# A two-layer diffusion backbone on one core: half vectors of the modulation turned four at a time, and a second top-16 selection over 112 candidates with larger lookups

## The chip, the cores and the metric

One core of a Trainium2 chip runs the whole network as one program. The metric is the device time of one execution in microseconds (us). Three executions of the kernel before took 3133.66, 3143.14 and 3145.10 us; their median is 3143.14 us. One more execution was profiled.

## The reference, cut to what matters

Two layers work on 256 noisy tokens (x) and 256 context tokens, each 1024 wide, in float32. Each layer is a modulated norm, an input projection, three token mixers with gates and an output projection, and then a modulated norm and an expert layer (PEER). Two parts matter here.

The **modulation**: a vector of 6 x 1024 values for each of the two conditioning vectors (x and context).

```python
def _modulation(cvec, w_mod, b_mod):
    m = jax.nn.silu(cvec) @ w_mod + b_mod
    return jnp.split(m[:, None, :], 6, axis=-1)
```

The **routing** of the expert layer: for each token and each of 8 heads two top-16 lists of 128 keys (the first selection), then the top 16 of the 16 x 16 sums of both lists (the second selection), whose places are looked up in the two lists of indices.

```python
    sv, si = lax.top_k(s, PEER_TOPK)
    cand = (sv[..., 0, :, None] + sv[..., 1, None, :]).reshape(B, L, PEER_HEADS, PEER_TOPK * PEER_TOPK)
    cidx = (si[..., 0, :, None] * N_KEYS + si[..., 1, None, :]).reshape(B, L, PEER_HEADS, PEER_TOPK * PEER_TOPK)
    top_s, pos = lax.top_k(cand, PEER_TOPK)
    eidx = jnp.take_along_axis(cidx, pos, axis=-1)
    gate = jax.nn.softmax(top_s, axis=-1)
```

Both lists are sorted from large to small. A pair (a, b) with (a+1)(b+1) > 16 has at least 16 pairs that are no smaller, so the 16 best lie among the pairs with a < 4 (4 x 16 = 64) and those with a >= 4 and b < 4 (12 x 4 = 48).

## The kernel before, in words

The program is a list of Python generators that are stepped against each other; a tile framework then gives every instruction its place on its engine and every tile its buffer, in the order of the program as far as the data are ready. A tile that is asked for while all buffers of its tag are held waits for one to come free. The pool of tag `f2` has 15 buffers of 2 KB per partition (line 66); it holds small weights (`wraw`, line 73: the DFT, pooling, query and key matrices that `front` loads), attention tiles, the one-hot tiles `e` of `gates`, the split activations of the experts and the padded vectors of the modulation. `f1` has 6 buffers of 1 KB.

Every large weight comes by DMA as a 256 KB piece (`raw`), ScalarE (ACT) rounds it to a high half (line 83), and VectorE (DVE) subtracts to get the low half (line 84); TensorE (PE) makes each product as three (lines 93 to 95).

**Modulation** (`mod_steps`, line 169). For each of the 6 parts and each half of 512 columns, 16 products (lines 183, 184) of a padded 128 x 128 tile, of which 4 columns are used (the high and low halves of two conditioning vectors), give 4 rows of 512. ACT copies the 4 rows (line 190). One half later `mod_out` (line 195) turns them into columns: 4 products with a 4 x 2 matrix (line 199, each shown as two records), an add of the bias (line 201), and for two parts one more operation (line 205). There are 24 halves in all: 4 before the first norm, 8 during the first front, 2 before the first expert layer, 4 during it and 6 around the last front.

**Fronts.** `front` (line 359) is a token mixer: a start with products of the loaded small matrices, 8 heads of attention (line 423 on), then two projections. It runs three times: (0,0) for the context, (0,1) for x of layer 0, (1,1) for layer 1. Inside each head it steps a generator `extra` six times. That is the modulation in fronts (0,0) and (1,1), and the routing of the context tokens (`early_routes`, line 930: two second selections) in front (0,1).

**Routing.** `scores` (line 514) makes the key scores and the first selections (`top16` on 128 values). `topk` (line 556) is the second selection for 128 tokens; it runs six times. For each of the 8 heads it makes 256 sums (line 562), and `top16` (lines 549 to 554) does MAX8, FIND_INDEX8 and MATCH_REPLACE8, then MAX8 and FIND_INDEX8 again, over all 256; each index or replace operation is preceded by a small MATCH_VALUE_LOAD. Then, for both lists (w) and four groups of 32 choices, three operations look up the index: compare with 0..15 (line 586), multiply by the list (line 589), sum over the 16 places (line 591). `topk` yields twice for each head and once for each of the 8 lookups, 24 times.

`routes` (line 939), once for each layer, weaves `topk` and `gates` (one-hot products that spread the gates over the experts: lines 628, 632 on DVE, 638 on PE) with `early`, which does a part of the experts' first products ahead of time (`down`, line 701: 24 products, two splits on DVE) at fixed rates per yield (0.36, 0.26, 0.22 and 0.53, 0.40, 0.32 products of 128 experts). The expert layers (`experts_both`, `experts_one`) follow.

Of the kernel before, what the change touches and what calls it, by code (L numbers as in the profile page):

```python
# [22 lines left out]
NH = 8  # L23
# [18 lines left out]
class Net:  # L42
# [22 lines left out]
    def f2(self, shape, dt=F32):  # L65
        return self.f.tile(shape, dt, name="f2", tag="f2", bufs=15)
# [36 lines left out]
    def setup(self):  # L103
        nc, c, h = self.nc, self.c, self.h

        def ld(name, shape):
            t = c.tile(shape, F32, name=name)
            nc.sync.dma_start(t, h[name])
            return t

        self.cv = ld("cv", [128, 8, 2])
        self.bmod = ld("bmod", [128, 2, 6, 8])
        self.hH = c.tile([128, 8, TT], F32R, name="hH")
        self.hL = c.tile([128, 8, TT], F32R, name="hL")
        self.ckvn = c.tile([128, TT], F32, name="ckvn")
        self.kr = c.tile([128, TT], F32, name="kr")

        z = c.tile([128, 8, 4], F32, name="z")
        sg = c.tile([128, 8, 2], F32, name="sg")
        nc.scalar.activation(sg, self.cv, AF.Sigmoid)  # L120
        nc.vector.tensor_mul(z[:, :, 0:2], sg, self.cv)
        sh = c.tile([128, 8, 2], F32R, name="sh")
        nc.vector.tensor_copy(sh, z[:, :, 0:2])
        nc.vector.tensor_sub(z[:, :, 2:4], z[:, :, 0:2], sh.bitcast(F32))
        self.sc4 = c.tile([128, 8, 4], F32, name="sc4")
        nc.vector.tensor_copy(self.sc4, z)
        self.sel = ld("sel", [4, 2])
        for l in range(2):
            self.mods[l] = c.tile([128, 6, 8, 2], F32, name=f"mods{l}")
            for w in (1, 2):  # L130
                self.AB[l, w] = c.tile([128, 8, 2], F32, name=f"ab{l}{w}")
# [12 lines left out]
    def setup2(self):  # L144
# [21 lines left out]
        self.iota16 = c.tile([128, 16], BF, name="iota16b")  # L166
        nc.vector.tensor_copy(self.iota16, it[:, 0:16])

    def mod_steps(self, l, *parts):
        nc, late = self.nc, None  # L170
        for part in parts:
            sc = [self.f2([128, 4, 128], F32R) for _ in range(2)]
            for i in range(2):
                nc.vector.memset(sc[i].bitcast(F32), 0.0)
                nc.vector.tensor_copy(sc[i][:, :, 0:4], self.sc4[:, 4 * i:4 * i + 4, :])
            yield
            for q in range(2):
                p = self.acc([128, 512])
                c0 = part * D + q * 512
                for k in range(8):  # L180
# [4 lines left out]
                    if k == 3 and late:  # L185
                        self.mod_out(l, *late)
                    if k % 2 and k < 7:
                        yield
                m4 = self.f2([4, 512])
                nc.scalar.copy(m4, p[0:4, :])  # L190
                late = part, q, m4
                yield
        self.mod_out(l, *late)

    def mod_out(self, l, part, q, m4):
        nc = self.nc
        mp = self.mm([128, 4, 2])
        for n in range(4):
            nc.tensor.matmul(mp[:, n, :], lhsT=m4[:, n * 128:(n + 1) * 128], rhs=self.sel, start=True, stop=True)
        ns = slice(4 * q, 4 * q + 4)  # L200
        nc.vector.tensor_tensor(self.mods[l][:, part, ns], mp,
                                self.bmod[:, l, part, ns].unsqueeze(2).to_broadcast([128, 4, 2]), op=OP.add)
        if q and part in (1, 4):
            g = self.g1 if part == 1 else self.g2
            nc.vector.scalar_tensor_tensor(self.AB[l, 1 if part == 1 else 2], self.mods[l][:, part], 1.0,
                                           g[:, l, :].unsqueeze(2).to_broadcast([128, 8, 2]),
                                           op0=OP.add, op1=OP.mult)
# [348 lines left out]
    def topk(self, sv, si, out):  # L556
# [3 lines left out]
        for hd in range(NH):  # L560
            cd = self.f1([128, 16, 16])
            nc.vector.tensor_tensor(cd, sv[:, 2 * hd, :].unsqueeze(2).to_broadcast([128, 16, 16]),
                                    sv[:, 2 * hd + 1, :].unsqueeze(1).to_broadcast([128, 16, 16]), op=OP.add)
            scr = self.f1([128, 256])
            yield from self.top16(ts[:, hd, :], pos[:, hd * 16:(hd + 1) * 16], cd.rearrange("p a b -> p (a b)"), scr)
            yield
        sb = kp.tile([128, 16, 16], BF, name="sb", bufs=1)
        nc.vector.tensor_copy(sb, si)
# [7 lines left out]
        pu = kp.tile([128, 2, 128], U32, name="pu", bufs=1)  # L576
        nc.vector.tensor_scalar(pu[:, 0, :], pos, 4, None, op0=OP.logical_shift_right)
        nc.vector.tensor_scalar(pu[:, 1, :], pos, 15, None, op0=OP.bitwise_and)
        pb = kp.tile([128, 2, 128], BF, name="pb", bufs=1)
        nc.vector.tensor_copy(pb, pu)  # L580
        ij = kp.tile([128, 2, 128], F32, name="ij", bufs=1)
        for w in range(2):
            for h2 in range(4):
                ks = slice(32 * h2, 32 * h2 + 32)
                oh = self.f1([128, 32, 16], BF)
                nc.vector.tensor_tensor(oh, self.iota16.unsqueeze(1).to_broadcast([128, 32, 16]),
                                        pb[:, w, ks].unsqueeze(2).to_broadcast([128, 32, 16]), op=OP.is_equal)
                o4 = oh.rearrange("p (h k) a -> p h k a", h=2)
                nc.vector.tensor_tensor(o4, o4, sb[:, 4 * h2 + w:4 * h2 + 4:2, :].unsqueeze(2).to_broadcast(
                    [128, 2, 16, 16]), op=OP.mult)  # L590
                nc.vector.reduce_sum(ij[:, w, ks], oh, axis=AX.X)
# [415 lines left out]
def _constants():  # L1007
# [28 lines left out]
    sel = np.array([[1, 0], [0, 1], [1, 0], [0, 1]])  # L1036
# [66 lines left out]
```

## Time and profile before

| what | value |
|---|---|
| median of three runs | 3143.14 us (3133.66 to 3145.10) |
| the profiled execution's own time | 3146.14 us |
| its span, first to last instruction | 3144.4 us |
| mean granted clock of TensorE | 0.965 |
| busy share of the span: PE, DVE, ACT, POOL | 94%, 81%, 46%, 10% |
| chain that ended last, by engine | PE 65%, DVE 17%, DMA 11%, issue 5%, ACT 2% |

How to read it: a busy share is an average over stages with different limits, so the stages have to be read one by one. The record of a DVE operation overlaps the start of the next one by some 0.08 us (the compare of line 586 has records of 681 ns, and two of them take 1.20 us on the chain); the pieces of the chain of waits show what an operation adds when another one follows it, and those are used for sums. A matmul's record overlaps its neighbours too, so a PE that is shown busy is not PE at its peak.

### The profile page before, as it was taken

To read this page: it belongs to the slowest core of one execution; us is meant where nothing else is said; L and a number is where in the kernel's file an instruction comes from. 1 tells how busy PE (TensorE), PEld (TensorE's weight loads), DVE (VectorE), ACT (ScalarE), POOL (GpSimd) and SP (SyncE) were. 2 spreads that over 40 slices of the span, in tenths; PEclk is the share of its full clock that TensorE was granted. 3 is DMA by queue.
4 is the path that set the end of the run, shared out by engine and by line. 5 is a ranking of instruction groups with operands and counts; after the bars stand their busy time and mean duration, and the time that the engine had idled before them with its cause. 6 is when DMAs were issued, how large, how long until landed. Compare 5 with 4: busy or idle time off the path is not lost.

```text
span 3144.4 us, 55017 instructions
## 1 busy us (share of the span) xinstructions
PE 2945.8 (94%) x19215; PEld 2726.3 (87%) x19215; DVE 2534.3 (81%) x5831; ACT 1460.3 (46%) x2814; POOL 323.9 (10%) x260
## 2 busy tenths in 40 slices
PE   7999899798898999999999999999988889999998
PEld 5799878798888889999999998789877877799997
DVE  6677889798997889899999998566799966666666
ACT  5565444443444443344334434445544544555554
POOL 0000000111000121433333341000000000000000
PEclk8999999899999999999999999999998999999999
DMA  7574443675568878898988986454546788776664
GB/s 233 179 230 142 145 126 111 203 242 194 179 185 251 303 250 273 303 307 305 304 303 304 320 291 214 143 160 142 185 143 186 218 264 278 242 231 205 208 201 141
DMA packets 400719, 695.36 MB, mean 221 GB/s; under 512 B 36793, under 2 KB 148153, under 8 KB 396345
## 3 DMA queue, kind: packets, MB, share of 16 engines
q1 hardware_dynamic: 363576, 557.61, 54.8%
q0 software_dynamic: 36864, 134.23, 12.8%
q8 instruction: 151, 2.47, 0.3%
q14 instruction: 128, 1.04, 0.1%
HBM read 631.94 MB, written 59.77 MB: 220 GB/s over the span
## 4 chain that ended last, share of the span: by engine, by line
PE 65%; DVE 17%; DMA 11%; issue 5%; ACT 2%; SPq 0%; POOL 0%; DVEq 0%; ACTq 0%
PE mm L93 9%; PE mm L94 8%; PE mm L95 8%; PE acc L94 7%; PE acc L95 7%; PE acc L93 7%; DVE wl L84 4%; DMA ge<-E 2%; PE acc L818 2%; PE acc L819 2%; PE acc L817 2%; DVE a L632 2%; DMA raw<-in_up 2%; DMA raw<-in_wmod 1%; DVE f L628 1%
## 5 line engine op out<-in xcount | busy, mean ns | idle before, releaser
L83 ACT CAST wh<-raw 128x512 fp32r<-128x512 f32 x1604 | 981.4, 619 | 1006.4 <-PE acc L95 267.4
L84 DVE TENSOR_TENSOR wl<-raw,wh 128x512 fp32r<-128x512 f32 x1604 | 1075.7, 685 | 276.4 <-ACT wh L83 264.4
L93 PE MATMUL mm<-hH,wh 128*128 128x256 f32 (+1 forms) x2432 | 760.0, 313 | 43.1 <-ACT ge L707 38.9
L94 PE MATMUL mm<-hH,wl 128*128 128x256 f32 (+1 forms) x2432 | 757.1, 311 | 19.8 <-DVE wl L84 18.8
L95 PE MATMUL mm<-hL,wh 128*128 128x256 f32 (+1 forms) x2432 | 751.6, 309 | 0.0
L93 PEld LDWEIGHTS mm<-hH,wh 128*128 128x128 f32 x2432 | 468.3, 193 | 52.2 <-ACT ge L707 44.7
L94 PEld LDWEIGHTS mm<-hH,wl 128*128 128x128 f32 x2432 | 469.3, 193 | 28.6 <-DVE wl L84 25.6
L95 PEld LDWEIGHTS mm<-hL,wh 128*128 128x128 f32 x2432 | 468.7, 193 | 0.0
L94 PE MATMUL acc<-f,wl 128*128 128x384 f32 (+1 forms) x1216 | 402.1, 331 | 7.3 <-DVE wl L84 6.9
L95 PE MATMUL acc<-f,wh 128*128 128x384 f32 (+1 forms) x1216 | 400.4, 330 | 1.9 <-DVE f L731 1.9
L93 PE MATMUL acc<-f,wh 128*128 128x384 f32 (+1 forms) x1216 | 394.1, 330 | 8.0 <-ACT wh L83 2.9
L669 POOL DMA_INDIRECT gx<-in_down,eidx x128 | 184.6, 1442 | 1030.7 <-ACT f L250 573.7
L93 PEld LDWEIGHTS acc<-f,wh 128*128 128x128 f32 x1216 | 230.5, 190 | 14.2 <-issue 6.4
L94 PEld LDWEIGHTS acc<-f,wl 128*128 128x128 f32 x1216 | 232.3, 191 | 11.3 <-DVE wl L84 10.8
L95 PEld LDWEIGHTS acc<-f,wh 128*128 128x128 f32 x1216 | 232.1, 191 | 2.5 <-DVE f L731 2.2
L707 ACT ACTIVATE ge<-mm 128x384 f32<-128x384 f32 (+1 forms) x256 | 111.8, 437 | 241.6 <-PE mm L95 219.6
L728 DVE TENSOR_TENSOR ge<-ge,f 128x256 f32<-128x256 f32 (+1 forms) x384 | 132.6, 375 | 99.5 <-ACT ge L707 50.3
L93 PE MATMUL acc<-hH,wh 128*128 128x256 f32 x688 | 210.4, 306 | 1.3 <-ACT hH L280 1.2
L818 PE MATMUL acc<-wl,f 128*128 128x512 f32 x512 | 202.8, 396 | 7.5 <-DVE wl L84 7.2
L817 PE MATMUL acc<-wh,f 128*128 128x512 f32 x512 | 201.1, 393 | 1.0 <-ACT f L730 1.0
L819 PE MATMUL acc<-wh,f 128*128 128x512 f32 x512 | 200.8, 392 | 0.0
L94 PE MATMUL acc<-hH,wl 128*128 128x256 f32 x688 | 198.6, 289 | 0.1
(207 smaller groups left out, 4496.8 us busy)
## 6 DMA issues: line engine op xcount, KB each, us to landing
raw<-in_downT SPq DMA_DIRECT2D x512, 256.0 KB
raw<-in_up SPq DMA_DIRECT2D x512, 256.0 KB
raw<-in_wmod SPq DMA_DIRECT2D x192, 256.0 KB
raw<-in_winc SPq DMA_DIRECT2D x172, 256.0 KB
G<-f SPq DMA_DIRECT2D x40, 1024.0 KB
f<-G SPq DMA_DIRECT2D x32, 1024.0 KB
raw<-in_wpq SPq DMA_DIRECT2D x96, 256.0 KB
raw<-in_wo SPq DMA_DIRECT2D x48, 256.0 KB
```

Of the source, the lines that this page charges most:

```text
L83: nc.scalar.copy(H, r)
L84: self.last = nc.vector.tensor_sub(L, r, H.bitcast(F32)).ins
L93: t.matmul(out, lhsT=wH, rhs=xH, start=first, stop=False)
L94: t.matmul(out, lhsT=wL, rhs=xH, start=False, stop=False)
L95: t.matmul(out, lhsT=wH, rhs=xL, start=False, stop=last)
L632: nc.vector.tensor_tensor(a, e[:, 0:4].unsqueeze(1).to_broadcast([128, 3, 4, 64, 2]), gT[:, t0 // 4].rearrange("p (x t) d -> p x t d", x=3 ...
L669: nc.gpsimd.indirect_dma_start(out=r, out_offset=None, in_=self.h["up"][0] if up else self.h["down0"], in_offset=bass.IndirectOffsetOnAxis ...
L707: nc.scalar.activation(a, p, AF.Gelu_apprx_tanh)
L728: nc.vector.tensor_mul(y, y, Gg[:, :, c, :])
L817: m(p[t][half], lhsT=aH[:, a], rhs=H[:, 0], start=(i == 0), stop=False)
L818: m(p[t][half], lhsT=aH[:, a], rhs=L[:, 0], start=False, stop=False)
L819: m(p[t][half], lhsT=aL[:, a], rhs=H[:, 0], start=False, stop=(i == 127))
```

## The change

It has two halves.

In the modulation the four used columns are written four times into the padded tile, 32 columns apart, so that the product gives the 4 rows at rows 0, 32, 64 and 96. ACT copies 32 rows of the half's own quarter into one fixed 128 x 512 tile `m4`, and `mod_out` runs once for up to four halves: 4 products with a 128 x 8 selection matrix, then one add for each half. The fixed tile takes the place of one of the 15 `f2` buffers.

In `topk` the 256 sums become 112 (64 + 48) for each head, made for four heads by two operations; `top16` runs over 112. The lookups are made for 64 choices at a time with the 16 places ahead of the choices in memory, so the sum reads with a step of 16 elements. The places come out of the position in 112 by two more shifts and three small operations. The list of indices `sb` is written with every value twice, side by side. The sums, the one-hot tiles and `pu` move from `f1` and the routing pool to `f2`. A yield stands before and after each of the 4 sums, so `topk` still yields 24 times.

```diff
-        return self.f.tile(shape, dt, name="f2", tag="f2", bufs=15)
+        return self.f.tile(shape, dt, name="f2", tag="f2", bufs=14)
...
-        self.sel = ld("sel", [4, 2])
+        self.sel = ld("sel", [128, 8])
+        self.m4 = c.tile([128, 512], F32, name="m4")
+        nc.vector.memset(self.m4, 0.0)
...
-        self.iota16 = c.tile([128, 16], BF, name="iota16b")
-        nc.vector.tensor_copy(self.iota16, it[:, 0:16])
+        self.iota16 = c.tile([128, 16, 16], BF, name="iota16b")
+        nc.vector.tensor_copy(self.iota16, it[:, 0:16].unsqueeze(2).to_broadcast([128, 16, 16]))
...
-                nc.vector.tensor_copy(sc[i][:, :, 0:4], self.sc4[:, 4 * i:4 * i + 4, :])
+                nc.vector.tensor_copy(sc[i].rearrange("p k (r c) -> p k r c", r=4)[:, :, :, 0:4],
+                                      self.sc4[:, 4 * i:4 * i + 4, :].unsqueeze(2).to_broadcast([128, 4, 4, 4]))
...
-                    if k == 3 and late:
-                        self.mod_out(l, *late)
+                    if k == 3 and len(late) == 4:
+                        self.mod_out(l, late)
+                        late = []
...
-                m4 = self.f2([4, 512])
-                nc.scalar.copy(m4, p[0:4, :])
-                late = part, q, m4
+                c = 32 * (len(late) % 4)
+                nc.scalar.copy(self.m4[c:c + 32, :], p[c:c + 32, :])
+                late.append((part, q))
...
-        mp = self.mm([128, 4, 2])
+        mp = self.mm([128, 4, 4, 2])
         for n in range(4):
-            nc.tensor.matmul(mp[:, n, :], lhsT=m4[:, n * 128:(n + 1) * 128], rhs=self.sel, start=True, stop=True)
+            nc.tensor.matmul(mp[:, n].rearrange("p a b -> p (a b)"), lhsT=self.m4[:, n * 128:(n + 1) * 128],
+                             rhs=self.sel, start=True, stop=True)
+        for i, (part, q) in enumerate(halves):
...
-        for hd in range(NH):
-            cd = self.f1([128, 16, 16])
-            nc.vector.tensor_tensor(cd, sv[:, 2 * hd, :].unsqueeze(2).to_broadcast([128, 16, 16]),
-                                    sv[:, 2 * hd + 1, :].unsqueeze(1).to_broadcast([128, 16, 16]), op=OP.add)
-            scr = self.f1([128, 256])
-            yield from self.top16(ts[:, hd, :], pos[:, hd * 16:(hd + 1) * 16], cd.rearrange("p a b -> p (a b)"), scr)
-            yield
-        sb = kp.tile([128, 16, 16], BF, name="sb", bufs=1)
-        nc.vector.tensor_copy(sb, si)
+        for h4 in range(2):
+            cd = self.f2([128, 4, 112])
+            ra, rb = sv[:, 8 * h4:8 * h4 + 8:2, :], sv[:, 8 * h4 + 1:8 * h4 + 8:2, :]
+            nc.vector.tensor_tensor(cd[:, :, 0:64].rearrange("p h (a b) -> p h a b", a=4),
+                                    ra[:, :, 0:4].unsqueeze(3).to_broadcast([128, 4, 4, 16]),
+                                    rb.unsqueeze(2).to_broadcast([128, 4, 4, 16]), op=OP.add)
+            nc.vector.tensor_tensor(cd[:, :, 64:112].rearrange("p h (a b) -> p h a b", a=12),
+                                    ra[:, :, 4:16].unsqueeze(3).to_broadcast([128, 4, 12, 4]),
+                                    rb[:, :, 0:4].unsqueeze(2).to_broadcast([128, 4, 12, 4]), op=OP.add)
+            for i in range(4):
+                hd = 4 * h4 + i
+                scr = self.f1([128, 112])
+                yield from self.top16(ts[:, hd, :], pos[:, hd * 16:(hd + 1) * 16], cd[:, i, :], scr)
+                yield
+        sb = kp.tile([128, 2, 128, 2], BF, name="sb", bufs=1)
+        for d in range(2):
+            nc.vector.tensor_copy(sb.rearrange("p w (h a) d -> p w h a d", h=8)[:, :, :, :, d],
+                                  si.rearrange("p (h w) a -> p w h a", w=2))
...
-        pu = kp.tile([128, 2, 128], U32, name="pu", bufs=1)
+        pu = self.f2([128, 4, 128], U32)
         nc.vector.tensor_scalar(pu[:, 0, :], pos, 4, None, op0=OP.logical_shift_right)
-        nc.vector.tensor_scalar(pu[:, 1, :], pos, 15, None, op0=OP.bitwise_and)
+        nc.vector.tensor_scalar(pu[:, 1, :], pos, 2, None, op0=OP.logical_shift_right)
+        nc.vector.tensor_scalar(pu[:, 2, :], pos, 15, None, op0=OP.bitwise_and)
+        nc.vector.tensor_scalar(pu[:, 3, :], pos, 3, None, op0=OP.bitwise_and)
         pb = kp.tile([128, 2, 128], BF, name="pb", bufs=1)
-        nc.vector.tensor_copy(pb, pu)
+        nc.vector.scalar_tensor_tensor(pb[:, 0, :], pu[:, 1, :], -12.0, pu[:, 0, :], op0=OP.add, op1=OP.max)
+        nc.vector.scalar_tensor_tensor(pb[:, 1, :], pu[:, 0, :], 4.0, pu[:, 2, :], op0=OP.is_lt, op1=OP.mult)
+        nc.vector.tensor_tensor(pb[:, 1, :], pb[:, 1, :], pu[:, 3, :], op=OP.max)
         ij = kp.tile([128, 2, 128], F32, name="ij", bufs=1)
         for w in range(2):
-            for h2 in range(4):
-                ks = slice(32 * h2, 32 * h2 + 32)
-                oh = self.f1([128, 32, 16], BF)
-                nc.vector.tensor_tensor(oh, self.iota16.unsqueeze(1).to_broadcast([128, 32, 16]),
-                                        pb[:, w, ks].unsqueeze(2).to_broadcast([128, 32, 16]), op=OP.is_equal)
-                o4 = oh.rearrange("p (h k) a -> p h k a", h=2)
-                nc.vector.tensor_tensor(o4, o4, sb[:, 4 * h2 + w:4 * h2 + 4:2, :].unsqueeze(2).to_broadcast(
-                    [128, 2, 16, 16]), op=OP.mult)
-                nc.vector.reduce_sum(ij[:, w, ks], oh, axis=AX.X)
+            for h4 in range(2):
+                ks = slice(64 * h4, 64 * h4 + 64)
+                oh = self.f2([128, 4, 16, 16], BF)
+                nc.vector.tensor_tensor(
+                    oh, self.iota16.unsqueeze(1).to_broadcast([128, 4, 16, 16]),
+                    pb[:, w, ks].rearrange("p (h k) -> p h k", h=4).unsqueeze(2).to_broadcast([128, 4, 16, 16]),
+                    op=OP.is_equal)
+                o4 = oh.rearrange("p h a (k d) -> p (h a) k d", d=2)
+                nc.vector.tensor_tensor(o4, o4, sb[:, w, ks, :].unsqueeze(2).to_broadcast([128, 64, 8, 2]), op=OP.mult)
+                yield
+                nc.vector.reduce_sum(ij[:, w, ks].rearrange("p (h k) -> p h k", h=4),
+                                     oh.rearrange("p h a k -> p h k a"), axis=AX.X)
                 yield
```

## Rows read from the trace of the kernel before

**Rows 1.** The page, part 1: busy time and share of each engine.

```profile
PE 2945.8 (94%) x19215; PEld 2726.3 (87%) x19215; DVE 2534.3 (81%) x5831; ACT 1460.3 (46%) x2814; POOL 323.9 (10%) x260
```

**Rows 2.** Busy time by stretch: first front, second front, then four stretches of routing.

```profile
core 0: us, PE busy (x) PEld busy (x) DVE busy (x) ACT busy (x) POOL busy (x), PEclk, DMA share, GB/s
115.00:290.00 175.00, 174.93 (x1278) 164.58 (x1277) 127.92 (x294) 105.10 (x220) 0.00 (x0) 1.00 0.62 196
460.00:575.00 115.00, 106.42 (x779) 95.12 (x779) 110.12 (x304) 49.37 (x103) 1.07 (x1) 1.00 0.35 110
768.00:837.00 69.00, 61.88 (x419) 59.81 (x420) 68.42 (x183) 27.68 (x49) 0.00 (x0) 0.95 0.57 176
837.00:928.00 91.00, 78.38 (x656) 72.97 (x654) 89.58 (x186) 39.24 (x68) 0.00 (x0) 0.94 0.59 175
2303.00:2350.00 47.00, 36.04 (x248) 33.89 (x249) 47.00 (x145) 16.89 (x32) 0.00 (x0) 0.85 0.44 143
2350.00:2464.00 114.00, 95.56 (x876) 90.91 (x875) 106.73 (x228) 51.65 (x97) 0.00 (x0) 0.90 0.63 194
```

**Rows 3.** Chain of waits, one second selection: start, us on the chain, what.

```profile
2302.96 0.18 DVE sv L553
2303.15 0.39 DVE f L551
2303.54 0.27 DVE si L554
2303.81 0.31 DVE tsc L553
2304.13 0.26 DVE scr L551
...
2307.99 0.41 DVE pos L554
...
2308.58 0.32 DVE f L562
...
2331.80 0.61 DVE ij L591
2332.41 0.20 DVE gate L575
2332.61 1.20 DVE f L586 x2
2333.81 0.67 DVE f L589 x2
```

**Rows 4.** Chain of waits, the gates' compare of 1024 elements.

```profile
2352.51 0.60 DVE f L628
```

**Rows 5.** Groups by line and form: ACT copies from PSUM, strided (L641) and plain (L388).

```profile
L641 ACT COPY f<-acc 128x512 f32<-128x512 f32 x160 | 91.5, 587 | 68.9 <-PE acc L638 66.7
...
L388 ACT COPY f<-acc 128x512 f32<-128x512 f32 x6 | 3.5, 587 | 4.5 <-PE acc L386 4.5
```

**Rows 6.** Chain of waits, whole span: a small load, head starts, a gather.

```profile
402.78 3.88 DMA f<-in_poolw
...
469.69 1.98 PE acc L444 x4
...
506.59 1.72 PE acc L444 x4
...
576.90 7.88 DMA gx<-in_down,eidx
...
2107.42 1.72 PE acc L444 x4
...
2123.46 1.72 PE acc L444 x4
```

**Rows 7.** Chain of waits in the first front: one turning of a half vector.

```profile
164.53 0.98 PE mm L199 x8
```

**Rows 8.** Groups by line and form: the experts' rounding into f2 tiles.

```profile
L730 ACT CAST f<-ge 128x384 fp32r<-128x384 f32 x128 | 65.1, 512 | 70.5 <-DVE ge L728 68.9 <-issue 0.9 <-ACT wh L83 0.7
```

More of the change, by code (lines that the diff above doesn't have):

```diff
@@ L165, in setup2 @@
         nc.vector.tensor_copy(self.iota.rearrange("p a b -> p (a b)"), it)
-        self.iota16 = c.tile([128, 16], BF, name="iota16b")
-        nc.vector.tensor_copy(self.iota16, it[:, 0:16])
+        self.iota16 = c.tile([128, 16, 16], BF, name="iota16b")
+        nc.vector.tensor_copy(self.iota16, it[:, 0:16].unsqueeze(2).to_broadcast([128, 16, 16]))
     def mod_steps(self, l, *parts):
-        nc, late = self.nc, None
+        nc, late = self.nc, []
         for part in parts:
@@ L192, in mod_steps, with mod_out @@
+                nc.scalar.copy(self.m4[c:c + 32, :], p[c:c + 32, :])
+                late.append((part, q))
                 yield
-        self.mod_out(l, *late)
-    def mod_out(self, l, part, q, m4):
+        self.mod_out(l, late)
+    def mod_out(self, l, halves):
         nc = self.nc
-        mp = self.mm([128, 4, 2])
+        mp = self.mm([128, 4, 4, 2])
         for n in range(4):
-            nc.tensor.matmul(mp[:, n, :], lhsT=m4[:, n * 128:(n + 1) * 128], rhs=self.sel, start=True, stop=True)
[L200 to L207, printed above, removed]
+            nc.tensor.matmul(mp[:, n].rearrange("p a b -> p (a b)"), lhsT=self.m4[:, n * 128:(n + 1) * 128],
+                             rhs=self.sel, start=True, stop=True)
+        for i, (part, q) in enumerate(halves):
+            ns = slice(4 * q, 4 * q + 4)
+            nc.vector.tensor_tensor(self.mods[l][:, part, ns], mp[:, :, i],
+                                    self.bmod[:, l, part, ns].unsqueeze(2).to_broadcast([128, 4, 2]), op=OP.add)
+            if q and part in (1, 4):
+                g = self.g1 if part == 1 else self.g2
+                nc.vector.scalar_tensor_tensor(self.AB[l, 1 if part == 1 else 2], self.mods[l][:, part], 1.0,
+                                               g[:, l, :].unsqueeze(2).to_broadcast([128, 8, 2]),
+                                               op0=OP.add, op1=OP.mult)
@@ L1035, in _constants @@
             dup[q, 64 + r] = 1.0
-    sel = np.array([[1, 0], [0, 1], [1, 0], [0, 1]])
+    sel = np.zeros((128, 8))
+    for q in range(4):
+        for r in range(4):
+            sel[32 * q + r, 2 * q + r % 2] = 1.0
     iota = np.broadcast_to(np.arange(128)[None, :], (128, 128))
```

## The prediction, made before the change was run

> **What bounds the kernel now.** I read the page first: over the whole span PE is busy 94%, DVE 81% [rows 1]. That is a mean over unlike stages, so I next read the busy time by stretch [rows 2]. In the first front PE is busy all 175 us and DVE 128: PE sets the end. In the second front, where the context's two second selections run beside attention, both are near full (PE 106 of 115, DVE 110). In the four stretches of routing, one for each second selection of `routes`, DVE is full: 68.4 of 69, 89.6 of 91, 47.0 of 47 and 106.7 of 114 us, and PE waits for it, for 7.1, 12.6, 11.0 and 18.4 us. [...]
>
> So time taken from DVE counts almost whole in the four routing stretches, little in the second front, and time taken from PE counts in the first and last front. The chain of waits gives the price of one DVE operation while others queue behind it [rows 3, 4].
>
> **The change, part by part: one second selection.** All on DVE, in us on the chain.
>
> *Selection.* Over 256 values MAX8 takes 0.31, FIND_INDEX8 with its load 0.41, MATCH_REPLACE8 with its load 0.39; over 128 values 0.18, 0.27 and 0.26 [rows 3]. A head costs 2 x 0.31 + 2 x 0.41 + 0.39 = 1.83 now and would cost 1.16 at 128. A value costs (0.31 - 0.18) / 128 = 0.001, so 112 values save another 5 x 0.016 = 0.08: 1.08. Eight heads save 8 x 0.75 = 6.0.
>
> *Sums.* Eight adds of 256 elements at 0.32 are 2.6 [rows 3]. In their place stand two of 256 (4 heads x 64) and two of 192, which lie between 0.20 (128 elements, L575) and 0.32: 0.26. 1.16 in all; saved 1.4.
>
> *Lookups.* Eight times compare 0.60, multiply 0.335 and sum 0.61 are 12.4 [rows 3]. After it there are four rounds on 1024 elements. The compare before reads one index again and again; after it both inputs run through neighbouring 16-bit elements, as in the gates' compare, whose 1024 elements take 0.60 [rows 4]. The upper bound is 1.12 (L586's 0.60, and 512 more at 0.001 each). I take 0.60, since form, type and size are those of that row. The multiply now does 512 in 0.335; it keeps pairs of neighbours and I take 0.60, again up to 1.12. The sum does 512 in 0.61, so 1024 take 0.61 + 0.52 = 1.13. Four rounds: 4 x 2.33 = 9.3; saved 3.0.
>
> The sum's input now steps by 16 elements, 32 bytes. No DVE row of before reads SBUF like that. The nearest row is ACT's copy of the gates' products, which reads PSUM with a step of 512 bytes: 587 ns for 512 elements, and 587 ns too for a plain copy of the same size [rows 5]. A step alone cost nothing there, so I take 1.13; the other end is below. [...] The row is of another engine and memory, so it doesn't settle this.
>
> *Small ones.* One more copy of the index list (at most 0.32), two more shifts (at most 0.20 each) and three 128-element operations at 0.20 for a copy of 256 at about 0.3: 1.0 more.
>
> One second selection thus saves 6.0 + 1.4 + 3.0 - 1.0 = **9.4 us** of DVE. The yields are 24 before and after, so the ahead-of-time products keep their places and number.
>
> *Where it counts.* A routing stretch gets shorter until PE's waits are used up: 7.1 in the first, 9.4 in each of the other three [rows 2]. **35 us.** The products, DMAs and gates of these stretches stay; what is late next is PE, waiting for the weights' low halves.
>
> *Second front.* DVE loses 2 x 9.4, but a head there is paced by PE. In the last front, which has no selection beside it, a head takes 2123.46 - 2107.42 = 16.0. In the second front two heads take 506.59 - 469.69 = 36.9, so 4.8 are lost [rows 6]; that is what comes back. After the last head the expert gather waits 7.88 us for its rows [rows 6], and it starts when the second selection has its last index; between 0 and 7.9 can come back, and I take 4.
>
> *One buffer less.* The fixed tile takes one of 15 `f2` buffers, and sums, one-hots and `pu` now use this pool too. Where a front starts, the small loads already wait for buffers: one pooling matrix stood 3.88 us on the chain [rows 6]. I charge one more such load, 3.9; bounds are 0 and three (11.6), one for each front. In the expert layers ACT's rounding into `f2` waits for DVE (68.9 of 70.5 us) and never for a product to free a buffer [rows 8]: nothing there. Second front and buffer together: 4.8 + 4 - 3.9 = **5 us** saved.
>
> **The modulation.** 24 turnings become 7: the generators hold 4, 8, 2, 4, 4 and 2 halves, so 1 + 2 + 1 + 1 + 1 + 1. One costs PE 0.98 [rows 7]. Six of the 17 that go lie in the first front and three in the last, where PE sets the end: 8.8. The other eight stand where loads or DVE share the bound; they are worth 0 to 7.8, and I take 3. The product behind a turning, 128 rows in place of 4, streams 8 columns in place of 2 and loads as many weights: nothing. ACT copies 32 rows in place of 4 in the same time, as its price goes by the 512 columns. Wider fills of the padded tile and the clearing of `m4` lie beside loads. Before the first norm four adds now stand in a row in place of one: 3 x 0.2 = 0.6 more, nothing covers them. **11 us** saved.
>
> **Sum.** 35 + 5 + 11 = 51 us. The profiled execution took 3146.1, so 3095 by its own clock; it stands 3 us above the median of the runs, and on the median the forecast is **3092 us**.
>
> **Rivals.**
> 1. *The strided sum is slow.* If each element of the sum costs double, a round costs 1024 x 0.001 = 1.04 more and a selection 4.2: it saves 5.2, the routing stretches 21, the whole 37: 3106. For it: no row here shows such a read on DVE. Against: the copies of [rows 5]. 0.17. [...]
> 2. *The next bound takes over.* DVE gets free, and the weights' loads or ACT set the pace. For: the last stretch has 7.3 us of idle DVE already and the DMA engines are at 0.44 to 0.63 [rows 2]. Against: ACT is under half busy, and the raw buffers come free with DVE's subtraction, so earlier. With half of 35 and only the 9 us of PE: 17 + 3 + 9 = 29 us, 3114. 0.17.
> 3. *The wide compare or multiply runs one element at a time.* 0.52 more each, 4.2 a selection for both: 3106. Against: the gates' compare [rows 4]. 0.05.
> 4. *Slower: the fronts starve for `f2` buffers.* SP issues in order, so a small load that waits for a buffer also holds the large weights behind it. The sums are held over 8 yields, more than one head, in a front that had little to spare. One exposed load is 3.88 [rows 6], and a front has 13 of them, 39 in three. The 51 us are used up by 13 exposed loads, and it becomes slower by 0.5% (16 us) from 17 on; with 20 it gives 3170. Against: four of the six selections run outside the fronts, and the loads run ahead of their use. 0.05.
>
> **How the numbers follow.** The forecast has 0.53; what is left, 0.03, is for another order of the instructions, which the framework chooses anew. About 0.5%, 16 us, is what a measurement of this kernel can tell from no change. The range: down to 3074 if the gather's wait, all turnings and the first stretch pay in full (4 + 5 + 2 more, and some of the idle PE clock back); up to 3120, rival 2 with a buffer's cost on top. Faster by more than 0.5% (below 3127) is the forecast and nearly all of rivals 1 to 3: 0.86. Within 0.5%: rivals 1 and 2 together, or half of rival 4: 0.09. Slower: 0.05.
>
> **What would show it.** In the profile after: MAX8 of the second selection near 0.25 us a record, compare and multiply of 1024 near 0.68, the sum near 1.2 (1.2 or more above that is rival 1); turning records 56 in place of 192; the four routing stretches shorter by 7 to 9 us each with DVE still near full; heads of the second front all at 16 us. If DVE has idle time there and the stretches are no shorter, rival 2 holds; if SP waits long for products at small loads, rival 4. A routing part that is under 20 us shorter in sum makes the forecast wrong.

## The result, and the profile of the changed kernel

The change made the kernel faster: 3109.0 us (median of six, 3102.0 to 3113.6) where the kernel before took 3144.1 beside it; ratio **0.988** [0.987, 0.990], or 35 us. In a second and a third group of runs the ratio was 0.991 [0.989, 0.993] and 0.988 [0.986, 0.990]. The forecast was 3092: the direction held, and 16 of the 51 us didn't come. The profiled execution took 3105.2 us, with a span of 3103.2.

First the page, part 1, which answers to [rows 1]:

```profile
PE 2911.3 (94%) x19079; PEld 2702.1 (87%) x19079; DVE 2500.5 (81%) x5766; ACT 1460.2 (47%) x2814; POOL 337.7 (11%) x260
```

DVE lost 33.8 us of busy time, where six selections at the forecast's 9.4 would have been 56. Next the groups by line and form, of DVE, for the operations of one second selection (before the bar: busy time in us and mean ns of a record):

```profile
L615 DVE TENSOR_REDUCE ij<-f 128x64 f32<-128x1024 bf16 x24 | 50.2, 2092 | 0.0
...
L613 DVE TENSOR_TENSOR f<-f,sb 128x1024 bf16<-128x1024 bf16 x24 | 16.2, 686 | 0.0
L608 DVE TENSOR_TENSOR f<-iota16b,pb 128x1024 bf16<-128x1024 bf16 x24 | 16.1, 681 | 0.0
...
L555 DVE MAX8 tsc<-f 128x8 f32<-128x112 f32 x48 | 12.2, 264 | 0.0
```

MAX8, compare (L608) and multiply (L613) have records of 0.26, 0.68 and 0.69 us, near the forecast's 0.25, 0.68 and 0.68. The sum (L615) takes 2.09 where 1.2 was forecast. On the chain of waits, start and us, two rounds of the third routing stretch answer to the last lines of [rows 3]:

```profile
2298.15 0.60 DVE f L608
...
2298.89 0.67 DVE f L613
...
2301.23 2.18 DVE ij L615
2303.41 0.60 DVE f L608
...
2304.54 0.67 DVE f L613
...
2305.74 2.07 DVE ij L615
```

The modulation's turnings, by their line (L203 is L199 of before, [rows 7]):

```profile
L203 PE MATMUL mm<-sel,m x56: 170/257/382, 47.9 to 2192.7; 128*128 128x8 f32 x56
```

56 records instead of 192, as forecast. The products with 128 rows have a median of 257 ns where those with 4 rows had 246 (L199 of before), their weight loads take 192 where they took 187, and ACT's copies of 32 rows of 512 take 576 where those of 4 rows took 572.

Now the time by stretch. For this I cut every profile at the same marks: the last record of the first selections, then the record that makes the gather's indices (the second front, with two second selections); and the last record of a layer's first selections, then the last gate product (the routing of layer 0 and of layer 1, with two second selections each). Busy time by these three windows, and by the rest of the span behind them, of the kernel before:

```profile
core 0: us, PE busy (x) PEld busy (x) DVE busy (x) ACT busy (x) POOL busy (x), PEclk, DMA share, GB/s
403.00:572.60 169.60, 159.41 (x1112) 138.37 (x1111) 149.95 (x426) 72.83 (x153) 0.00 (x0) 1.00 0.37 115
778.00:987.50 209.50, 192.15 (x1594) 180.90 (x1591) 206.75 (x433) 91.06 (x162) 0.00 (x0) 0.97 0.63 190
2309.20:2524.40 215.20, 184.29 (x1730) 173.91 (x1731) 207.78 (x431) 99.11 (x187) 0.00 (x0) 0.92 0.62 191
2524.40:3144.40 620.00, 592.48 (x3506) 519.74 (x3503) 385.69 (x708) 325.96 (x643) 0.00 (x0) 0.99 0.69 222
```

and of the changed kernel:

```profile
396.30:557.40 161.10, 154.10 (x1084) 135.62 (x1083) 136.78 (x397) 70.57 (x149) 0.00 (x0) 1.00 0.38 119
762.20:966.60 204.40, 189.07 (x1580) 178.61 (x1580) 195.47 (x414) 92.61 (x165) 0.00 (x0) 0.97 0.64 197
2283.10:2483.10 200.00, 173.20 (x1717) 165.19 (x1718) 196.46 (x411) 97.87 (x185) 0.00 (x0) 0.96 0.66 205
2483.10:3103.20 620.10, 595.81 (x3507) 525.93 (x3504) 387.01 (x709) 326.53 (x643) 0.00 (x0) 0.98 0.68 221
```

In both layers DVE was relieved of the same: 206.75 - 195.47 = 11.3 and 207.78 - 196.46 = 11.3 us, 5.65 a selection. Layer 0's routing got only 5.1 us shorter for it, layer 1's 15.2. In layer 0 DVE now idles 9 of 204 us where it idled 3; in layer 1 it idles 3.5 of 200 where it idled 7.4. In layer 1 the granted TensorE clock rose too, from 0.92 to 0.96 of full speed, and PE was busy 11 us less (with 1717 products where 1730 lay in the window). But the clock isn't what made this stretch shorter. The kernel before with one buffer less, which is among the experiments below, got 0.95 there, with PE busy 179 us, and the stretch took 213.9 us, 1.3 under the 215.2 of before:

```profile
2310.40:2524.30 213.90, 178.64 (x1728) 168.85 (x1729) 207.56 (x432) 98.98 (x187) 0.00 (x0) 0.95 0.62 192
```

The last experts take what they took.

### The profile page after: what moved, and what is told of

It is laid out like the page before. It is cut to its first block, busy times and chain, and to the rows that moved or that the text cites. A ratio compares the mean times of both kernels' runs of the same rounds, so it can differ in the third digit from the quotient of the medians.

```text
span 3103.2 us, 54692 instructions
## 1 busy us (share of the span) xinstructions
PE 2911.3 (94%) x19079; PEld 2702.1 (87%) x19079; DVE 2500.5 (81%) x5766; ACT 1460.2 (47%) x2814; POOL 337.7 (11%) x260
## 3 DMA queue, kind: packets, MB, share of 16 engines
q14 instruction: 127, 1.04, 0.1%
## 4 chain that ended last, share of the span: by engine, by line
PE 63%; DVE 18%; DMA 11%; issue 5%; ACT 2%; POOL 0%; SPq 0%; DVEq 0%; ACTq 0%; POOLq 0%
PE mm L93 8%; PE mm L94 8%; PE mm L95 8%; PE acc L95 6%; PE acc L94 6%; PE acc L93 6%; DVE wl L84 4%; PE acc L843 3%; PE acc L842 3%; PE acc L844 3%; DVE a L657 2%; DMA ge<-E 2%; DMA gx<-in_up,eidx 2%; DVE xT L812 2%; DMA raw<-in_up 2%
## 5 line engine op out<-in xcount | busy, mean ns | idle before, releaser
L84 DVE TENSOR_TENSOR wl<-raw,wh 128x512 fp32r<-128x512 f32 x1604 | 1077.6, 686 | 291.7 <-ACT wh L83 280.3
L694 POOL DMA_INDIRECT gx<-in_down,eidx x128 | 197.3, 1541 | 1011.8 <-DVE f L505 558.2
L843 PE MATMUL acc<-wl,f 128*128 128x512 f32 x512 | 202.3, 395 | 5.4 <-DVE wl L84 5.3
L842 PE MATMUL acc<-wh,f 128*128 128x512 f32 x512 | 201.7, 394 | 0.4 <-ACT f L755 0.4
L694 POOL DMA_INDIRECT gx<-in_up,eidx x128 | 140.2, 1095 | 552.9 <-DVE av L707 448.5
```

Of the source, the lines that this page charges most:

```text
L84: self.last = nc.vector.tensor_sub(L, r, H.bitcast(F32)).ins
L694: nc.gpsimd.indirect_dma_start(out=r, out_offset=None, in_=self.h["up"][0] if up else self.h["down0"], in_offset=bass.IndirectOffsetOnAxis ...
L842: m(p[t][half], lhsT=aH[:, a], rhs=H[:, 0], start=(i == 0), stop=False)
L843: m(p[t][half], lhsT=aH[:, a], rhs=L[:, 0], start=False, stop=False)
```

## The experiments

Two things were to be told apart: what the sum costs and why, and whether DVE's time still is the routing's time. The table has every profile cut at the marks above; "rest" is what is left of the span. Where a kernel was profiled more than once, each value stands, so that the spread shows: a window varies by 1 to 3 us between profiles of one kernel, the rest by 7.

| kernel | second front | routing, layer 0 | routing, layer 1 | rest |
|---|---|---|---|---|
| before | 169.6 | 209.5 | 215.2 | 2550 |
| before, 14 buffers | 169.4 | 209.6 | 213.9 | 2546 |
| modulation alone | 170.5 | 211.9 | 215.3 | 2538 |
| routing alone | 161.7 | 202.8 | 199.7 | 2552 |
| whole change | 161.1, 163.4, 162.2 | 204.4, 204.7, 202.7 | 200.0, 201.0, 201.7 | 2538, 2543, 2542 |
| sum reads neighbours | 158.7 | 204.7 | 196.9 | 2547 |
| halving additions | 155.3, 154.5 | 202.5, 202.3 | 195.8, 193.3 | 2547, 2540 |
| strided sum twice | 182.5 | 214.6 | 215.0 | 2551 |

### The parts of the change

The modulation alone keeps the change's edits there, with the routing of before; the other is the reverse, with the pool of before:

```diff
-        return self.f.tile(shape, dt, name="f2", tag="f2", bufs=14)
+        return self.f.tile(shape, dt, name="f2", tag="f2", bufs=15)
```

> The modulation of the change alone, with the routing of before and 14 buffers. Theory (the parts add up, and the modulation counts in three fronts): 8 to 14 us less than before, about 3133 us, a ratio of 0.9955 to 0.9975; the four routing stretches as before within 2 us. Rival (the fronts are bound elsewhere, and what was seen there belongs to the routing's lead): within 4 us of before. The routing stretches tell too whether the lost buffer costs anything there.

> The routing of the change alone, with the modulation of before and 15 buffers. Theory: 21 to 25 us less than before, about 3121 us, a ratio of 0.992 to 0.9935, nearly all of it between the first selections and the last gate product of each layer. Rival (the lost buffer holds back the routing of layer 0, which gained 5.1 us where layer 1 gained 16.4): with 15 buffers layer 0 gains 10 us or more, and the kernel comes to 3112 or less, no slower than the whole change.

Modulation alone: ratio 0.998 [0.996, 0.999], 7 us (2 to 12). That is under the 8 to 14 that I expected, and the interval leaves room for the rival's "within 4 us". Its windows are those of before within 3 us, and the rest is 8 to 12 us shorter in its one profile. Routing alone: 0.992 [0.990, 0.995], 24 us, as expected; in its one profile the windows are 30 us shorter and the rest isn't. Layer 0 gained 6.7 us there and not the rival's 10. 7 and 24 make 31, where the change gave 35, 29 and 40 in its three groups of runs: the parts add up. With 15 buffers layer 0's routing is no shorter than with 14 (202.8 beside 202.7 to 204.7), so the buffer isn't what holds it. That was tried by itself too, in the kernel before:

```diff
-        return self.f.tile(shape, dt, name="f2", tag="f2", bufs=15)
+        return self.f.tile(shape, dt, name="f2", tag="f2", bufs=14)
```

> The kernel before with 14 buffers of f2 where it had 15, nothing else. Theory (the lost buffer is a small term, 3.9 us in the forecast's sum): 0 to 6 us over the kernel before. Rival (it is what holds back layer 0's routing): 8 us or more over it, and layer 0's four hundred microseconds from the second front to the last gate product 5 us longer or more.

1.000 [0.999, 1.001]: in the routing of before the lost buffer costs nothing.

### What the sum costs: the same reduction over neighbours

The sixteen places of a value now lie side by side, so that the sum, still one instruction of 1024 values, reads neighbours; compare and multiply keep pairs, and the positions are doubled by two small copies.

```diff
-                oh = self.f2([128, 4, 16, 16], BF)
+                oh = self.f2([128, 64, 8, 2], BF)
...
-                nc.vector.reduce_sum(ij[:, w, ks].rearrange("p (h k) -> p h k", h=4),
-                                     oh.rearrange("p h a k -> p h k a"), axis=AX.X)
+                nc.vector.reduce_sum(ij[:, w, ks], oh.rearrange("p k a d -> p k (a d)"), axis=AX.X)
```

> The sum stays one instruction of 1024 values with 64 outputs, but the places lie innermost, so that it reads neighbours; compare and multiply keep pairs of equal size. Two small copies per selection (about 0.2 us each) double the positions. Theory (the stride costs, not the reduction): a sum of about 1.1 to 1.2 us where it was 2.09, 4 x 0.95 - 0.3 = 3.5 us per selection, 14 for the four, about 3095 us. Rival (a reduction of 1024 bf16 values costs some 2 us however it reads): the sum's record stays at 2.0 or more, and the time at 3107 to 3112. If compare or multiply rise above 0.75 us, the layout of the pairs costs there what the sum gives, and the records say how much.

Group by line and form of that kernel:

```profile
L615 DVE TENSOR_REDUCE ij<-f 128x64 f32<-128x1024 bf16 x24 | 29.0, 1213 | 0.0
...
L612 DVE TENSOR_TENSOR f<-f,sb 128x1024 bf16<-128x1024 bf16 x24 | 16.2, 685 | 0.0
```

**1.213 us against 2.092** for the same values, count and result: reading with the step costs 0.88 us per 1024 values, and without it the forecast's 1.2 was right. The rival, by which a reduction of 1024 values takes 2 us however it reads, is out. Only these two were measured, a step of 32 bytes and none, so it isn't shown why the step costs, nor what another step would.

The time was 3099.2 us, ratio 0.986 [0.983, 0.989] beside 0.988 to 0.991 for the whole change in its three groups of runs. The interval overlaps with those of two of them; on the same chip the whole change took 3114.0, but in another group. 3095 was expected. Busy time by stretch, the two routings:

```profile
765.00:969.70 204.70, 189.13 (x1581) 178.47 (x1581) 189.69 (x415) 93.22 (x166) 0.00 (x0) 0.97 0.65 197
2296.00:2492.90 196.90, 174.08 (x1717) 165.89 (x1718) 190.58 (x414) 97.97 (x185) 0.00 (x0) 0.95 0.68 209
```

DVE is relieved of another 6 us in each. Layer 1 is 4 us shorter for it (and the second front 3), layer 0 not at all.

### Halving additions in place of the sum

```diff
-                nc.vector.reduce_sum(ij[:, w, ks].rearrange("p (h k) -> p h k", h=4),
-                                     oh.rearrange("p h a k -> p h k a"), axis=AX.X)
+                for n in (8, 4, 2):
+                    nc.vector.tensor_add(oh[:, :, 0:n], oh[:, :, 0:n], oh[:, :, n:2 * n])
+                nc.vector.tensor_add(ij[:, w, ks].rearrange("p (h k) -> p h k", h=4), oh[:, :, 0], oh[:, :, 1])
```

> The strided sum of each round (1024 values read 32 bytes apart, 2.09 us a record) gives way to four additions that halve the places, all with neighbouring 16-bit values: 512, 256, 128 and 64 outputs, about 0.34 + 0.22 + 0.15 + 0.15 = 0.8 to 0.9 us by the records of the products of 512 and 1024 values. Theory (the sum's stride is what the forecast mis-sized, and the routing stretches are VectorE's): 4 rounds x 1.2 = 5 us less per selection, 20 for the four; about 3090 us, the four routing stretches 4 to 6 us shorter each, a ratio to the kernel before of 0.981 to 0.984. Rival (the stretches have come to their next bound, ScalarE's copies and the weights, as the growth of VectorE's idle time from 2.7 to 8.9 us in layer 0's routing could mean): under 8 us less, 3101 or more, and the idle time grows by what the sums lose.

> The whole change beside the next three on one chip, since its ratio was 0.988 on one and 0.991 on another: 0.987 to 0.992.

> The halving additions again, on the chip of the whole change. By the stretches of the two profiles the shorter sums are worth 2 us in layer 0's routing, 5 in layer 1's and 8 in the second front, 15 of the 28 us that VectorE is spared. Theory (half of it counts, because layer 0's routing has come to its next bound): 8 to 16 us under the whole change on the same chip. Rival (all of it counts, and the first chip was unlike): 20 us or more. Other rival (the lead is given back in the experts, whose stretch was 4 to 8 us longer with the additions): under 5 us.

First 3099.8 us (0.986 [0.983, 0.989]); then, in one group of runs with the whole change, 3095.2 (0.984 [0.982, 0.986]) against 3106.0 (0.988 [0.986, 0.990]): **11 us** less, which five runs of each give to some 7 us. The first expectation of 20 fell; the second of 8 to 16 held, with its rivals (under 5, and 20 or more) at the edge of that uncertainty or beyond it. Busy time by stretch, second profile:

```profile
400.60:555.10 154.50, 152.72 (x1073) 134.19 (x1072) 127.42 (x418) 69.64 (x148) 0.00 (x0) 1.00 0.40 124
759.70:962.00 202.30, 187.54 (x1580) 177.10 (x1580) 186.31 (x438) 93.15 (x166) 0.00 (x0) 0.98 0.64 199
2280.70:2474.00 193.30, 170.92 (x1717) 163.91 (x1718) 187.13 (x435) 98.08 (x185) 0.00 (x0) 0.97 0.68 212
```

DVE is relieved of another 9 us in each window. The second front (-8) and layer 1 (-7) follow it, layer 0 (-1 to -2) doesn't: there DVE's idle time grows from 9 to 16 us instead. What it waits for shows in the waits of layer 0's routing (engine, line, what it waited for, us, times, longest), first a line of the kernel before, then the changed kernel:

```profile
PE acc L638 <- DVE a L632: 10.8, 14, 1.8
```

```profile
ACT wh L83 <- DMA raw<-in_downT: 21.7, 12, 5.3
ACT wh L83 <- PE mm L95: 19.4, 18, 2.5
...
PE acc L663 <- DVE a L657: 12.8, 15, 1.5
...
DVE wl L84 <- ACT wh L83: 5.3, 5, 1.8
```

with the additions:

```profile
ACT wh L83 <- DMA raw<-in_downT: 24.2, 12, 4.7
ACT wh L83 <- PE mm L95: 18.0, 17, 2.7
...
PE acc L664 <- DVE a L658: 12.8, 15, 1.5
DVE wl L84 <- ACT wh L83: 11.8, 9, 1.8
```

and with the strided sum issued twice, which is the next experiment:

```profile
PE acc L665 <- DVE a L659: 12.7, 15, 1.5
```

DVE's subtraction of the weights' halves (L84) waits for ACT's rounding, 11.8 us where it was 5.3 (and nothing before the change); ACT itself waits for the weights' load and for PE's expert products. PE's wait for the gates' multiply is 12.8, 12.8 and 12.7 us, with DVE busy 195, 186 and 211 us in the window: it is the gates' own chain, not the second selections, and neither relief nor more work of the selections moves it. Before the change it was 10.8 of PE's 17.4 idle us (13.0 of 20.9 in the profile with 14 buffers), so only some 7 were there for the selections to give back; in the changed kernel it is 12.8 of 15.3, and 2.5 are left. So PE is as near to being layer 0's next bound as ACT's order is; which of the two it is was only read from these waits and wasn't tried.

### The strided sum issued twice

```diff
                 nc.vector.reduce_sum(ij[:, w, ks].rearrange("p (h k) -> p h k", h=4),
                                      oh.rearrange("p h a k -> p h k a"), axis=AX.X)
+                nc.vector.reduce_sum(ij[:, w, ks].rearrange("p (h k) -> p h k", h=4),
+                                     oh.rearrange("p h a k -> p h k a"), axis=AX.X)
```

> The whole change once more, so that the others of this group stand beside it on one chip: a ratio to the kernel before of 0.987 to 0.990 by both theories, some 36 us.

> The whole change with the strided sum issued twice: 4 x 2.1 = 8.4 us more of VectorE per selection, 50 us over the six. Theory (layer 0's routing has come to the products of the early experts on TensorE, which is why taking 1.2 us from each sum shortened it by nothing; layer 1's is still VectorE's): layer 0's two stretches, with 8.9 us of VectorE's idle time to take up first, grow by 8 to 12 us of the 16.8, layer 1's by 13 to 17, the second front by 4 to 9 a selection; in sum 28 to 40 us over the change, 3137 to 3149. Rival (the sum's length is covered everywhere now): under 15 us over the change. Other rival (each stretch is VectorE's still, and the halving additions failed for another reason): 45 us or more.

3157.0 us (1.004 [1.002, 1.006] of before) beside 3114.0 of the whole change: **43 us** for 24 more sums. The ratio of the whole change in this group is 0.991, just above the 0.987 to 0.990 that I expected. The price of the sums, in the groups by line and form:

```profile
L615 DVE TENSOR_REDUCE ij<-f 128x64 f32<-128x1024 bf16 x24 | 49.9, 2078 | 0.0
L617 DVE TENSOR_REDUCE ij<-f 128x64 f32<-128x1024 bf16 x24 | 49.5, 2064 | 0.0
```

So 43 of 49.5 us counted: more than the 28 to 40 that I expected, under the 45 of the rival by which every stretch is DVE's. The runs give the 43 to some 6 us, so the time alone decides for neither; the stretches tell more. Busy time by stretch:

```profile
401.20:583.70 182.50, 164.91 (x1089) 142.10 (x1087) 154.05 (x409) 72.76 (x153) 0.00 (x0) 0.96 0.34 105
791.20:1005.80 214.60, 193.59 (x1579) 182.09 (x1579) 210.96 (x422) 92.34 (x165) 0.00 (x0) 0.95 0.61 186
2326.10:2541.10 215.00, 180.55 (x1717) 171.35 (x1718) 211.71 (x417) 98.34 (x185) 0.00 (x0) 0.92 0.61 191
```

Each window got 16.5 us of sums. Layer 1 grew by 14 and layer 0 by 11, both as expected; in layer 0 the other 5 came out of DVE's idle time, which fell from 9 to 4. The second front grew by 20, where at most 18 were expected. The changed kernel thus stands in layer 0 at the bend: work added to DVE counts for most of its length, work taken away for little.

### More expert work under layer 1's routing

With the additions DVE idles 6 to 8 us and PE 22 to 24 in the window of layer 1's routing. The early blocks of the experts' first product can fill that. The edit for 62 blocks (with 68 blocks the rates are 0.67, 0.5 and 0.4):

```diff
-EARLY0, EARLY1 = 48, 56
+EARLY0, EARLY1 = 48, 62
...
-SC0, SC1, R0, R1 = 0.5, 0.5, (0.36, 0.26, 0.22), (0.53, 0.4, 0.32)
+SC0, SC1, R0, R1 = 0.5, 0.5, (0.36, 0.26, 0.22), (0.6, 0.45, 0.36)
```

> The halving additions in place of the strided sum, and in layer 1 more of the expert work laid under the routing: 62 blocks early where it was 56, at rates of 0.6, 0.45 and 0.36. With the additions VectorE idles 9 us of the 201 of layer 1's routing, and TensorE 28. Theory (TensorE's idle time there is to be had, at 1.4 us of VectorE for the weights of a block): layer 1's routing 0 to 4 us longer, the last experts 9 to 14 us shorter, the kernel 5 to 10 us under that with the additions alone, about 3090 to 3095 us. Rival (VectorE is the bound there as soon as blocks are added): the stretch grows by what the experts lose, no difference within 4 us.

> The whole change with its strided sum, and 62 early blocks at the raised rates in layer 1. VectorE idles only 3.5 to 4.5 us of the 200 of layer 1's routing here. Theory (the blocks can lie there at all only because the additions made room on VectorE): layer 1's routing grows by 18 us or more and the kernel gains under 6 us on the whole change. Rival (TensorE's idle time is what they use, and VectorE's share doesn't matter): 10 to 15 us under the whole change, as much as the additions gained by it.

> The additions and 68 early blocks at rates of 0.67, 0.5 and 0.4 in layer 1. With 62 blocks VectorE still idled 13.6 us and TensorE 20.4 of the 208 of layer 1's routing. Theory: 0 to 6 us under 62 blocks, about 3083 us. Rival (the last part, which grew from 60 to 68 us, is full): 0 to 5 us over it.

These kernels ran in two groups, B and C, each on one chip; in B the whole change took 3114.0 us.

| kernel | time, us | ratio to before | routing, layer 1 | last experts |
|---|---|---|---|---|
| whole change, group C | 3106.0 | 0.988 [0.986, 0.990] | 201.7 | 616.2 |
| strided sum, 62 blocks, group C | 3104.0 | 0.987 [0.985, 0.989] | 211.4 | 602.7 |
| additions, group C | 3095.2 | 0.984 [0.982, 0.986] | 193.3 | 615.6 |
| additions, 62 blocks, group B | 3086.5 | 0.982 [0.980, 0.983] | 208.5 | 597.3 |
| additions, 68 blocks, group C | **3083.1** | **0.981** [0.979, 0.983] | 219.3 | 579.4 |

Under the strided sum the blocks bring nothing that can be told from none (2 us), though the routing grew by 10 and not by the 18 that I expected. Under the additions 68 blocks bring 12: the routing grows by 26 and the last experts shrink by 36; 62 blocks stand 27 us under the whole change of their group, where the additions alone stood 11 under it in theirs. My expectation for 62 blocks was wrong in its parts: the routing grew by 13 to 15 us and not by 0 to 4, the last experts lost some 18 and not 9 to 14, and the time came out under the expected 3090 to 3095. That 68 blocks are better than 62 isn't shown, since they ran in different groups with ratios of 0.981 and 0.982. That the blocks need the additions isn't shown to the end, since 68 blocks were not run with the strided sum. Of the version with 68 blocks, layer 1 and what follows it:

```profile
2273.40:2492.70 219.30, 201.11 (x1995) 194.44 (x1996) 203.25 (x460) 114.67 (x220) 0.00 (x0) 0.99 0.73 226
2492.70:3072.10 579.40, 558.66 (x3229) 488.10 (x3226) 367.80 (x685) 307.11 (x609) 0.00 (x0) 0.99 0.71 228
```

PE is busy 201 of 219 us where it was 171 of 193, at a clock of 0.99. This version beats both kernels in its group, before by 63 us and the whole change by 23.

## Why the prediction was right, and where it was wrong

**Selection, sums of candidates, small ones: right.** The sum reading neighbours shows it: there nearly everything else in the selection is as in the change, and DVE's relief in the two routings is 206.75 - 189.69 = 17.1 and 207.78 - 190.58 = 17.2 us, 8.6 a selection. It has two copies more (they double the positions) and one less (of the index list), each a record of 0.3 us, so with the change's own copies the relief would be some 8.9, where 9.4 was forecast.

**"I take 1.13", for the sum of a round: wrong, and the first of two causes.** The row on which I leaned, ACT's copy from PSUM [rows 5], is of another engine and another memory, and it didn't carry over. The sum measured 2.07 to 2.18 on the chain, 0.94 or more above 1.13; four rounds make 3.8 us, and 9.4 - 3.8 = 5.6 is what was measured. This was rival 1, to which I gave 0.17, with 5.2 a selection and 3106 us in all; the median is 3109. (The sign that I set for it, a record 1.2 us or more above the forecast, was higher than its own price of 1.04 a round, and the record stayed under it, at 0.9.)

**"Until PE's waits are used up", 35 us in four stretches: wrong in layer 0, and the second cause.** The routing gave 20 us on the mean of three profiles (5.6 and 14.3), right at the mark below which I had said the forecast would be wrong. Cut at the last lookup of each selection, the four stretches got 6, 2, 5 and 10 us shorter in the profile above, where 7 to 9 each were forecast, and layer 0 lost 2.6 again in the gates behind. The second is the one that failed, where the selection runs beside the gates of the first; before and after:

```profile
830.70:926.50 95.80, 83.18 (x680) 77.79 (x680) 93.79 (x203) 40.85 (x71) 0.00 (x0) 0.94 0.59 177
```

```profile
809.30:903.00 93.70, 83.37 (x696) 78.14 (x695) 90.14 (x196) 41.85 (x73) 0.00 (x0) 0.96 0.63 192
```

The price of the sum alone doesn't explain this: with the stride gone the two windows give 23 us for 34 of relief, with the additions 28 for 41, not 35. I had taken all of PE's idle time for waiting on the selections. In layer 0 10.8 of its 17.4 us were waiting for the gates' multiply, which stays, so there was room for some 7 us and not for 16.5; and DVE, once relieved, waits for ACT's rounding of the weights (5.3 us with the change and 11.8 with the additions, nothing before). A next bound thus took over in one layer of two, as rival 2 had it; that it is the weights' loads or ACT, as rival 2 says, and not PE itself, isn't shown. So rival 1's routing of 21 us came out nearly in sum, but as 6 and 14, not as two halves.

**Layer 1 gave more than DVE was relieved of** (14.3 on the mean for 11.3), which the forecast had only as a possibility at its low end, by the clock. No run shows that PE's waits cost clock which comes back with them, and the clock doesn't explain the surplus: at 0.92, 0.94 and 0.95 the routing of before took 215.2, 215.3 and 213.9 us. What else fell is DVE's idle time, 6.3 to 7.5 us in the three profiles with the routing of before and 3.0 to 5.0 in the four with that of the change. Some 2 us of it are waits of the gates' multiply for PE's products, of which these are the lines before and after:

```profile
DVE a L632 <- PE acc L638: 2.5, 3, 1.6
```

```profile
DVE a L657 <- PE acc L663: 0.4, 1, 0.4
```

Why PE was ready sooner is not shown.

**Second front and buffer, 5 us: about right in sum, by luck, and wrong in its parts.** The 4.8 us of the heads didn't come. On the chain of waits the first and the last head of the second front start, before and after, at

```profile
420.65 1.72 PE acc L444 x4
...
539.05 1.73 PE acc L444 x4
```

```profile
413.63 1.82 PE acc L450 x4
...
531.45 1.73 PE acc L450 x4
...
558.60 5.60 DMA gx<-in_down,eidx
```

118.4 us before and 117.8 after. The 7 to 8 us of the window lie behind the last head, where the second selection comes to its end: 34 us from that head to the window's end before, 26 after. The gather's wait, which lies behind the window, went from 7.9 us to 5.6, 7.0 and 7.2 in three profiles, so 1 to 2 came back where I took 4. The 3.9 charged for the buffer are nothing: 1.000 [0.999, 1.001] in the routing of before, and with the routing of the change the windows with 15 buffers are those with 14 within 2 us, and the rest is no shorter.

**Modulation, 11 us: the right way, with the size at the upper end of what was measured.** The 56 turnings are as forecast; alone it measured 7 us, 2 to 12. The six turnings of the first front were priced at 5.9 us: up to the end of the second front's first selections the three profiles without the new modulation took 401.1 to 404.7 us and the eleven with it 396.3 to 402.2, 3.4 less on the mean.

Rival 3 is out by the records of 0.68 and 0.69 us for compare and multiply; rival 4, a slower kernel, by the time and by the buffer that cost nothing.

In sum, 51 forecast against 35: the routing 15 short, the modulation 4, the second front 2 or 3 over. That the median came so near to rival 1's 3106 is in part luck, since layer 1's and the second front's surplus made up for what layer 0 and the modulation lacked.

## What to carry to other kernels

When many small instructions become few larger ones, price the larger one by its new access pattern, on its own engine and memory: here two fifths of a selection's gain were lost to a sum whose values lay 32 bytes apart, and putting them side by side, or adding halves onto each other, brought it back on the engine. And read the idle time of the waiting engine by what it waits for before counting it as room: only the part that waits for what the change shortens can be used up. Once an engine is relieved, the work laid beside it has to be set anew: twelve more early blocks, at raised rates, then gave as much as the better sum itself.

## What the hardware showed beyond that

- A sum on DVE over 1024 neighbouring bf16 values took 1.213 us, while compare and multiply of as many took 0.684 and 0.685 in the same profile: the one reduction cost nearly as much as both of them. Four halving additions of 512, 256, 128 and 64 outputs came to 0.41 + 0.28 + 0.22 + 0.21 = 1.12 us of records (0.8 to 0.9 were expected), hardly less than the one reduction. Two of their records, in the groups by line and form:

```profile
L616 DVE TENSOR_TENSOR f<-f 128x512 bf16<-128x512 bf16 x24 | 9.9, 411 | 0.0
...
L616 DVE TENSOR_TENSOR f<-f 128x256 bf16<-128x256 bf16 x24 | 6.8, 282 | 0.0
```

- The ratio of the whole change to the kernel before differed between groups of runs by about the width of its interval: 0.988, 0.991 and 0.988. A step of 10 us between kernels of different groups is therefore not told from none.
